# Layer-1 gates by row sums on VectorE, without GpSimd splits and gate sums, and with a shorter closing norm, in a two-layer hybrid block

## The chip, the cores and the metric

The kernel runs on 1 core of one Trainium2 chip. The metric is device time in microseconds (us) of one execution, the median of several runs; smaller is better. PE is TensorE (its matmuls; PEld is its weight loads), DVE is VectorE, ACT is ScalarE, POOL is GpSimd, SP is SyncE, which issues the DMAs here.

## The reference

Two layers over 256 context and 256 latent tokens of width 2048. A layer norms its input, modulates it with a shift and a scale, projects it, mixes it by two branches, projects back, norms again and adds the result times a gate. Shift, scale and gate come from a conditioning vector:

```python
cond_x = jax.nn.silu(c)
for i in range(DEPTH):
    sh_x, sc_x, gt_x = jnp.split(cond_x @ ada_w[i] + ada_b[i], 3, axis=-1)
    u_x = modulate(rms_norm(h_x, pre_g[i]), sh_x, sc_x)
    ...
    h_x = h_x + gt_x[:, None] * rms_norm(out_x, post_g[i])
```

The change touches how `gt_x` of layer 1 is computed (a vector of 2048 times a matrix of 2048 by 2048), where the residues of some weights are made, and the last norm, after which `h_x` is the output. Only the latent tokens are needed at the end of layer 1.

## The kernel before

Every large product is done as three matmuls of a split pair: a tile of weights (`raw`, 512 KB, 128 partitions by 1024 floats) is rounded to `wh` by ACT (line 73), the residue `wl` is made by DVE (line 76), and PE runs high by high, high by low, low by high (`mm3`, and line 469 in `group`). `group` takes eight such tiles of weights, one per pair of K blocks, from `next_w`, which keeps three ready. `raw` has four buffers, and every tile of conditioning weights (`ada`) shares them.

After each K pair `group` calls a step function, which pushes background work one step on: generators for the conditioning (`ada_steps`, `ada_vec`), for attention (`att`) and for the state-space branch (`s5q`). The order in which the engines get their instructions is made by the scheduler of the language from this program order and its own estimate of times, with `tc.high_priority()` as a hint; each engine then runs its list strictly in order.

The conditioning matrices are cut into 12 blocks of 512 columns for each layer, block q 8 to 11 being the gate. Three ways are in use:

- `ada_steps` on PE: the conditioning vector is the stationary side, the matrix streams through (line 143).
- `ada_vec` with `eng` V: DVE multiplies each K tile with its scalar and adds (line 387), PE sums over partitions at the end (line 398).
- `ada_vec` with `eng` G: ACT multiplies in place in the `raw` buffer (line 392), POOL adds (line 393), then the same sum on PE. Layer 1's gate blocks 9 to 11 go this way (line 1303); block 8 goes by `ada_steps` (line 909).

The places in order of time: layer 0 up to its last projection (`wo0`, four passes n4, lines 898 to 926); its last pass runs in two halves, t 0 and 1, then t 2 and 3, each followed by `mid_chain` (line 860), which norms the tokens on DVE and ACT so that the projections of layer 1 can start (`u1_pair`). In the second half of that pass five of the eight `wl` residues are made by POOL (lines 302 and 314). Then layer 1: one group for the state-space input, and from line 1318 six iterations over pairs of heads, each a group `kv` and a group `aq`/`ag` (in the first iteration `kv` ran earlier), with attention of the pair before and the state-space branch as background; `step1` (line 1305) runs the POOL generator from the second iteration on, and `step_ada` two times in three. A last projection (`adg`), then the closing stage: four passes of 512 columns over two token tiles (lines 1381 to 1393), the sums of squares on ACT, the gate product on DVE, and after the last pass `token_rsqrt` (line 850) and four updates with their output DMAs for each token tile.

Of the kernel before, what the change touches and what calls it, by code (L numbers as in the profile page):

```python
# [10 lines left out]
F32 = mybir.dt.float32  # L11
# [7 lines left out]
P = 128  # L19
# [21 lines left out]
def tile_backbone(ctx: ExitStack, tc: tile.TileContext, a):  # L41
# [225 lines left out]
    for q in range(8):  # L267
# [23 lines left out]
        for kt in (2 * q, 2 * q + 1):  # L291
# [7 lines left out]
    wsrc = [(a["w0"][i, kp], 512) for i in range(7) for kp in range(8)]  # L299
    wsrc += [(a["w0t"][kp], P) for kp in range(8)]  # L300
    wsrc += [(a["w0"][7, kp], 512) for kp in range(8)]
    wsrc += [(a[nm][i, kp], 512) + ((G,) if nm == "wo0" and n == 4 and kp in range(2, 7) else ())
             for nm, order in (("wo0", (0, 1, 2, 3, 3)),
                               ("w1", (0, 0) + tuple(range(1, 14))), ("wo1", (0, 1, 2, 3)))
             for n, i in enumerate(order) for kp in range(8)]
    wready = []

    def load_w(src, n, slo=V):
        w = wpool.tile([P, 2, 512], F32, tag="raw", name="raw", bufs=4)
        wh = wpool.tile([P, 2, 512], F32R, tag="wh", name="wh", bufs=3)  # L310
        wl = wpool.tile([P, 2, 512], F32R, tag="wl", name="wl", bufs=3)
        w, wh, wl = w[:, :, 0:n], wh[:, :, 0:n], wl[:, :, 0:n]
        nc.sync.dma_start(w, src)
        split(w, wh, wl, slo=slo)
        return wh, wl

    def fill_w(n):
# [51 lines left out]
            ada_finish(epool[0], l, q, es, epool[1])  # L369
            ada_done(l, (q,))  # L370

    def ada_vec(l, qs, nm, pool, eng):

        accs = []
        for i, q in enumerate(qs):
            accs += [pool.tile([P, 512], F32, tag="pa%d" % (i * nm + m), name="pa")
                     for m in range(nm)]
            for kp in range(8):
                w = wpool.tile([P, 2, 512], F32, tag="raw", name="raw", bufs=4)
                k0 = 2 * (kp % 2)  # L380
                nc.sync.dma_start(w, a["ada%d" % l][q, kp // 2][:, k0:k0 + 2, :])
                for kt, m in ((2 * kp + j, m) for j in range(2) for m in range(nm)):
                    acc, wj, c = accs[i * nm + m], w[:, kt % 2, :], condS[:, kt, m:m + 1]
                    if kt == 0:
                        S.activation(acc, wj, AF.Copy, scale=c)
                    elif eng is V:
                        V.scalar_tensor_tensor(acc, wj, c, acc, ALU.mult, ALU.add)  # L387
                    else:
                        pr = wj
                        if m < nm - 1:  # L390
                            pr = scr.tile([P, 512], F32, tag="t512", name="pr")
                        S.activation(pr, wj, AF.Copy, scale=c)  # L392
                        eng.tensor_tensor(acc, acc, pr, ALU.add)  # L393
                yield
        n = 32 * len(accs)
        E = psp.tile([P, 512], F32, tag="ps", name="Ep")
        for g, acc in enumerate(accs):
            T.matmul(E[32 * g:32 * g + 32, :], ones[:, 0:32], acc, start=True, stop=True,
                     skip_group_check=True)
        es = scr.tile([P, 512], F32, tag="t512", name="es")  # L400
        S.activation(es[0:n], E[0:n], AF.Copy)
        yield
        pt = psp.tile([P, 4, n], F32, tag="ps", name="ept")
        for b in range(4):
            T.transpose(pt[:, b, :], es[0:n, b * P:(b + 1) * P], ident[0:n, 0:n])
        for i, q in enumerate(qs):
            lo = COLS["adab"][0] + 48 * l + 4 * q
            V.tensor_tensor(
                ada[l][:, 4 * q:4 * q + 4, 0:nm],
                pt.rearrange("p b (q m r) -> p q r b m", q=len(qs), m=nm)[:, i, 0],  # L410
                cols[:, lo:lo + 4].rearrange("p (b o) -> p b o", o=1).to_broadcast([P, 4, nm]),
                ALU.add)
        ada_done(l, qs)

    gates = [0, 0]

    def ada_done(l, qs):
        for q in qs:
            if q < 8:
                mod_cols(l, q)  # L420
            else:
                gates[l] += 1
                if gates[l] == 4:
                    gate_rows(l, *epool)

    def run(q, n=1):
        while q and n > 0:
# [318 lines left out]
    kts = list(range(KT))  # L746
    for l, qs in ((0, range(8, 12)), (1, range(8))):
        ada_bg.append(ada_steps(l, [q for q in qs if (l, q) not in ((1, 5), (1, 6), (1, 7))]))
        pool_bg += [ada_vec(l, (q,), 2, l0, V) for q in qs if (l, q) in ((1, 5), (1, 6), (1, 7))]

    def step0():
        step_ada()
# [153 lines left out]
    pump(1e9)  # L906
    run(ada_bg, 1e9)
    run(pool_bg, 1e9)
    ada_bg.append(ada_steps(1, range(8, 12 - 3)))
    out0_open(3)  # L910
    pairs = iter(())

# [70 lines left out]
    ustr = lambda kt, j: (uh[kt].rearrange("p (c j) -> p j c", j=4)[:, j, :],  # L983
                          ul[kt].rearrange("p (c j) -> p j c", j=4)[:, j, :])
    accs, blocks = tblocks(ustr)
    group(kts, blocks, step=step_ada)
    U = l1.tile([P, 16, P], F32, tag="U", name="U")
    D2 = [l1.tile([P, 4, 4, 32], F32, tag=tg, name="D2" + tg) for tg in ("PT", "bias", "qT", "sg")]
    for j in range(4):
# [310 lines left out]
    s5q += [s5_inputs(), s5_pairs(), s5_glu()]  # L1300
    qs = P ** -0.5

    pool_bg = [ada_vec(1, tuple(range(12 - 3, 12)), 1, l1, G)]

    def step1():
        if hp_ >= 1:
            run(pool_bg)
        step_ada()
        run(att)
        run(s5q)  # L1310

# [34 lines left out]
    for k in KORD1[:2]:  # L1346
# [5 lines left out]
    while ada_bg:  # L1352
        step_ada()
    run(pool_bg, 1e9)
    run(s5q, 1e9)
    run(att, 1e9)
    for k in KORD1[2:8]:
# [16 lines left out]
    for c, tg in enumerate(("uh14", "ul14", "uh15", "ul15")):  # L1374
# [3 lines left out]
    oF = [[o0[:, c, :] for c in range(4)],  # L1378
          [l1.tile([P, 512], F32, tag=tg, name="o1" + tg) for tg in ("bias", "qT", "sg", "VT")]]
    ssf = l1.tile([P, 2, 4], F32, tag="ssf", name="ssf")  # L1380
    for n4 in range(4):
        accs = [acc_tile("ao%d" % t) for t in range(2)]
        group(KORD1, [blk(accs[t], 0, 512, sta=lambda k, t=t: ntok(k, t)) for t in range(2)],
              tail=3 if n4 == 3 else 1)
        for t in range(2):
            jk = scr.tile([P, 512], F32, tag="t512", name="jk")
            S.activation(jk, accs[t], AF.Square, accum_out=ssf[:, t, n4:n4 + 1])
            V.tensor_tensor(oF[t][n4], accs[t], g1[n4], ALU.mult)
            if n4 == 3:
                r = token_rsqrt(ssf[:, t:t + 1, :], 1, "rf%d" % t, "rf")  # L1390
                for c in range(4):
                    V.scalar_tensor_tensor(hx[t][c], oF[t][c], r, hx[t][c], ALU.mult, ALU.add)
                    nc.sync.dma_start(a["out"][t][:, 512 * c:512 * c + 512], hx[t][c])
# [3 lines left out]
def _ct(x):  # L1397
    return np.ascontiguousarray(x)
# [18 lines left out]
def _layout(inp):  # L1417
# [29 lines left out]
    for l in range(2):  # L1447
        aw = inp["ada_w"][l].reshape(4, 4, P, 6144)
        out = np.empty((12, 4, P, 4, 512), np.float32)
        for q in range(12):  # L1450
            out[q] = aw[:, :, :, qcols[q]].transpose(0, 2, 1, 3)
        o["ada%d" % l] = out
    w = inp["ab_w_in"][0]
    gv = lambda *cs: sum([[1024 + P * c, P * c] for c in cs], [])
    bg = lambda *cs: [4096 + P * c for c in cs]
# [59 lines left out]
```

## Time and profile before

| | |
|---|---|
| Time, median of 3 runs (lowest, highest) | 1566.83 us (1566.81, 1566.91) |
| The profiled execution's own time | 1562.3 us |
| Its span | 1560.5 us |
| Mean granted TensorE clock | 0.986 of full |
| Busy share of the span: DVE, ACT, POOL | 66%, 38%, 15% |
| Moved by DMA | 268.83 MB, mean 172 GB/s |

The span runs from the first to the last instruction; the execution's own time is 1.8 us longer. The profiled execution was 4.5 us faster than the median of the runs. Durations below are of this one execution.

### The profile page before, as it was taken

The page shows a single profiled execution, that of the slowest core. Times are in us where ns is not written, and L with a number is a line of the kernel's source. Part 1 is how long each engine was busy: PE and PEld are TensorE (multiplying, and loading weights), DVE is VectorE, ACT ScalarE, POOL GpSimd, SP SyncE. Part 2 cuts the span into 40 slices and gives each one's busy share as a digit, 9 for nine tenths or more (in the row PEclk, how much of TensorE's full clock was granted, in tenths as well). Part 3 has the DMA queues.
Part 4 walks back from the last instruction along what each step waited for, and adds up shares of the span by engine and source line. Part 5 has one row for each costly group of instructions (what it writes and reads, how often), then busy time and mean ns, then how long its engine had stood idle before and what let it go on. Part 6 is the DMA issues. An engine that isn't in the chain of part 4 may idle for free.

```text
span 1560.5 us, 22281 instructions
## 1 busy us (share of the span) xinstructions
PE 1476.7 (95%) x8306; PEld 1192.1 (76%) x8306; DVE 1026.0 (66%) x2364; ACT 599.0 (38%) x1162; POOL 241.2 (15%) x229
## 2 busy tenths in 40 slices
PE   3999999999999999999989998879999999999996
PEld 2557767777867767787669997668888979889884
DVE  5244999999675456554376638679597785635645
ACT  4222112122234133322358435664463554424542
POOL 0000000010030000000030116774243343100000
PEclk9999999999999999999999999989999999999998
DMA  9985444455344666654574445553232332425653
GB/s 388 359 319 210 162 162 160 164 174 171 122 154 155 205 229 215 209 169 135 188 248 139 149 142 178 188 166 119 75 126 85 112 102 88 142 81 176 229 190 108
DMA packets 74940, 268.83 MB, mean 172 GB/s; under 512 B 8352, under 2 KB 11984, under 8 KB 70096
## 3 DMA queue, kind: packets, MB, share of 16 engines
q1 hardware_dynamic: 74832, 267.42, 49.7%
q8 instruction: 65, 1.06, 0.3%
q14 instruction: 43, 0.35, 0.1%
HBM read 263.16 MB, written 4.22 MB: 171 GB/s over the span
## 4 chain that ended last, share of the span: by engine, by line
PE 71%; DVE 16%; DMA 6%; ACT 3%; issue 2%; POOL 2%; SPq 0%; DVEq 0%; ACTq 0%; POOLq 0%
PE acc L469 31%; PE kv L469 11%; PE ao L469 7%; DMA raw<-in_ada_dram 5%; PE E L143 5%; DVE wl L76 3%; PE acc L204 2%; PE aq L469 2%; PE ag L469 2%; PE acc L205 2%; PE adg L469 1%; PE acc L203 1%; PE po L1271 1%; POOL pa L393 1%; ACT wh L73 1%
## 5 line engine op out<-in xcount | busy, mean ns | idle before, releaser
L73 ACT ACTIVATE wh<-raw 128x1024 fp32r<-128x1024 f32 (+1 forms) x264 | 274.2, 1039 | 584.0 <-PE acc L469 254.8
L76 DVE TENSOR_TENSOR wl<-raw,wh 128x1024 fp32r<-128x1024 f32 (+1 forms) x259 | 324.5, 1255 | 231.0 <-ACT wh L73 230.3
L504 DVE SCALAR_TENSOR_TENSOR cv<-ain,cw,cv 128x512 f32<-128x512 f32 x240 | 170.1, 748 | 0.0
L469 PE MATMUL acc<-uh,wh 128*128 128x512 f32 x400 | 159.6, 399 | 1.6 <-ACT wh L73 1.1
L469 PE MATMUL acc<-uh,wl 128*128 128x512 f32 x400 | 155.3, 392 | 2.3 <-DVE wl L76 2.3
L469 PE MATMUL acc<-ul,wh 128*128 128x512 f32 x400 | 156.1, 390 | 0.0
L469 PE MATMUL kv<-wh,uh 128*128 128x256 f32 x384 | 109.3, 285 | 1.9 <-DVE sg L1316 1.9
L469 PE MATMUL kv<-wl,uh 128*128 128x256 f32 x384 | 109.3, 285 | 0.0
L469 PE MATMUL kv<-wh,ul 128*128 128x256 f32 x384 | 109.3, 285 | 0.0
L387 DVE SCALAR_TENSOR_TENSOR pa<-raw,condS,pa 128x512 f32<-128x512 f32 x90 | 63.2, 747 | 66.7 <-DMA raw<-in_ada_dram 60.8
L469 PEld LDWEIGHTS acc<-uh,wh 128*128 128x128 f32 x400 | 75.0, 188 | 38.9 <-ACT wh L73 10.0
L469 PEld LDWEIGHTS acc<-uh,wl 128*128 128x128 f32 x400 | 75.1, 188 | 20.4 <-DVE wl L76 2.7
L469 PEld LDWEIGHTS acc<-ul,wh 128*128 128x128 f32 x400 | 75.2, 188 | 15.5 <-issue 0.8
L469 PE MATMUL kv<-uh,wh 128*128 128x512 f32 (+1 forms) x224 | 85.8, 386 | 1.0 <-ACT uh L894 1.0
L469 PE MATMUL kv<-uh,wl 128*128 128x512 f32 (+1 forms) x224 | 81.7, 366 | 1.2 <-DVE wl L76 1.2
L469 PE MATMUL kv<-ul,wh 128*128 128x512 f32 (+1 forms) x224 | 81.0, 363 | 0.0
L393 POOL TENSOR_TENSOR pa<-pa,raw 128x512 f32<-128x512 f32 x45 | 65.9, 1467 | 87.3 <-ACT raw L392 84.8
L469 PEld LDWEIGHTS kv<-wh,uh 128*128 128x128 f32 x384 | 73.9, 192 | 4.3 <-DVE sg L1316 2.6
L469 PE MATMUL acc<-wh,mh 128*128 128x512 f32 x192 | 75.4, 395 | 1.6 <-DVE oG L848 1.6
L469 PE MATMUL acc<-wh,uh 128*128 128x512 f32 x192 | 76.1, 398 | 0.0
L469 PE MATMUL acc<-wl,uh 128*128 128x512 f32 x192 | 75.6, 394 | 0.0
L469 PE MATMUL acc<-wh,ul 128*128 128x512 f32 x192 | 75.5, 393 | 0.0
(393 smaller groups left out, 3440.2 us busy)
## 6 DMA issues: line engine op xcount, KB each, us to landing
raw<-in_w_dram SPq DMA_DIRECT2D x184, 512.0 KB, 3.4
raw<-in_ada_dram SPq DMA_DIRECT2D x128, 512.0 KB, 4.6
raw<-in_wo_dram SPq DMA_DIRECT2D x72, 512.0 KB, 3.4
aw<-in_ada_dram SPq DMA_DIRECT2D x32, 1024.0 KB, 7.0
w<-in_w0a_dram SPq DMA_DIRECT2D x8, 896.0 KB, 6.8
h<-in_h_dram SPq DMA_DIRECT2D x4, 1024.0 KB, 7.8
h0t<-in_h0t_dram SPq DMA_DIRECT2D x16, 256.0 KB, 4.4
bias<-in_bias_dram SPq DMA_DIRECT2D x12, 256.0 KB, 3.6
```

The source lines that it names most:

```text
L73: S.activation(hi, src, AF.Copy)
L76: slo.tensor_tensor(lo, src, hi.bitcast(F32), ALU.subtract)
L143: T.matmul(E[32 * g:32 * g + 32, :], condS[:, kt, :], raw, start=(kt < 4), stop=(kt >= 12), skip_group_check=True)
L203: T.matmul(ps, wh, xh, start=start, stop=False)
L204: T.matmul(ps, wh, xl, start=False, stop=False)
L205: T.matmul(ps, wl, xh, start=False, stop=stop)
L387: V.scalar_tensor_tensor(acc, wj, c, acc, ALU.mult, ALU.add)
L393: eng.tensor_tensor(acc, acc, pr, ALU.add)
L469: T.matmul(out, lt, rt, start=st and m == 0, stop=en and m == 2, skip_group_check=True)
L504: ins = V.scalar_tensor_tensor(o, x[:, :, k:k + L], cw05[:, ch, k:k + 1], o, ALU.mult, ALU.add)
L1271: T.matmul(po, vT[:, k, i * P:(i + 1) * P], U_["PT"][:, k, :], start=k == 0, stop=k == 3)
```

## The change

- Layer 1's gate no longer goes by `ada_steps` and `ada_vec`. The gate's weights are laid out with the 2048 output columns along partitions (16 blocks of 128) and the conditioning rows along the free axis, in two halves of 1024 (`ada1g`). For each half, the conditioning vector is spread over all partitions by one DMA (`crow`), and for each of 16 blocks one DVE instruction multiplies a `raw` tile with it and sums each row into one column of `gs`. That makes 32 loads of 512 KB and 32 DVE instructions of 128 by 1024, each with a read of its accumulator. The bytes stay the same: four blocks of 4 MB before, 32 of 512 KB after.
- The conditioning vector is written as a row to DRAM once, when layer 0's gates are ready (`cond_row`).
- `step1` runs `gate_sums` on every second step from the third iteration over heads on. The remaining part of it and `gate_rows` run after the `adg` group is listed.
- The block of gate 8 that PE did during the last pass of layer 0 goes, and the five POOL residues there are made by DVE.
- In the closing stage the sums of the first three passes and EPS are added ahead; the factor 1/D goes into the square; `rsqrt1` has two instructions in each round instead of three; squares, gate products and `rsqrt1` have high priority.

```diff
-    wsrc += [(a[nm][i, kp], 512) + ((G,) if nm == "wo0" and n == 4 and kp in range(2, 7) else ())
+    wsrc += [(a[nm][i, kp], 512)
...
-    def load_w(src, n, slo=V):
+    def load_w(src, n):
...
-        split(w, wh, wl, slo=slo)
+        split(w, wh, wl)
...
-                        pr = wj
-                        if m < nm - 1:
-                            pr = scr.tile([P, 512], F32, tag="t512", name="pr")
-                        S.activation(pr, wj, AF.Copy, scale=c)
-                        eng.tensor_tensor(acc, acc, pr, ALU.add)
...
+    def cond_row(psp, tag="ps"):
+
+        pc_ = psp.tile([16, P], F32, tag=tag, name="pct")
+        cc = scr.tile([P, KT], F32, tag="t512", name="cc")
+        V.tensor_copy(cc, condS[:, :, 0])
+        T.transpose(pc_, cc, ident)
+        cr = sp.tile([32, P], F32, tag="gr", name="cr")[0:16]
+        S.activation(cr, pc_, AF.Copy)
+        nc.sync.dma_start(crowd.rearrange("m (k f) -> (m k) f", f=P), cr)
+
+    def gate_sums(pool):
+
+        gs = pool.tile([P, 2, 16], F32, tag="gs", name="gs")
+        for hf in range(2):
+            cr = pool.tile([P, 1024], F32, tag="crow", name="crow")
+            nc.sync.dma_start(cr, crowd[0:1, 1024 * hf:1024 * hf + 1024].to_broadcast([P, 1024]))
+            for b in range(16):
+                w = wpool.tile([P, 2, 512], F32, tag="raw", name="raw", bufs=4)
+                w = w.rearrange("p j f -> p (j f)")
+                nc.sync.dma_start(w, a["ada1g"][hf, b])
+                V.tensor_tensor_reduce(w, w, cr, 1.0, 0.0, ALU.mult, ALU.add,
+                                       accum_out=gs[:, hf, b:b + 1])
+                yield
+        g = ada[1][:, 32:48, 0]
+        lo = COLS["adab"][0] + 80
+        V.tensor_tensor(g, gs[:, 0, :], gs[:, 1, :], ALU.add)
+        V.tensor_tensor(g, g, cols[:, lo:lo + 16], ALU.add)
+        gate_rows(1, psp)
...
-    ada_bg.append(ada_steps(1, range(8, 12 - 3)))
...
-    group(kts, blocks, step=step_ada)
+    group(kts, blocks)
...
-    pool_bg = [ada_vec(1, tuple(range(12 - 3, 12)), 1, l1, G)]
+    gate_bg = [gate_sums(l1)]
 
     def step1():
-        if hp_ >= 1:
-            run(pool_bg)
-        step_ada()
+        turns[0] += 1
+        if hp_ >= 2 and turns[0] % 2:
+            run(gate_bg)
...
+    def rsqrt1(v, v2, nm):
+
+        t, y, n_ = (l1.tile([P, 1], F32, tag=nm + x, name=nm + x) for x in "tyn")
+        V.tensor_scalar(n_, v, v2, None, ALU.add)
+        V.tensor_scalar(t.bitcast(I32), n_.bitcast(I32), 1, None, ALU.logical_shift_right)
+        V.tensor_scalar(y.bitcast(I32), t.bitcast(I32), -1, 0x5F3759DF, ALU.mult, ALU.add)
+        V.tensor_scalar(n_, n_, -0.5, None, ALU.mult)
+        for _ in range(3):
+            V.scalar_tensor_tensor(t, y, n_, y, ALU.mult, ALU.mult)
+            V.scalar_tensor_tensor(y, t, 1.5, y, ALU.add, ALU.mult)
+        return y
...
-            S.activation(jk, accs[t], AF.Square, accum_out=ssf[:, t, n4:n4 + 1])
-            V.tensor_tensor(oF[t][n4], accs[t], g1[n4], ALU.mult)
+            with tc.high_priority():
+                S.activation(jk, accs[t], AF.Square, scale=D ** -0.5,
+                             accum_out=ssf[:, t, n4:n4 + 1])
+                V.tensor_tensor(oF[t][n4], accs[t], g1[n4], ALU.mult)
+            if n4 == 2:
+
+                V.tensor_reduce(pre[:, t:t + 1], ssf[:, t, 0:3], axis=AX.X, op=ALU.add)
+                V.tensor_scalar(pre[:, t:t + 1], pre[:, t:t + 1], EPS, None, ALU.add)
             if n4 == 3:
-                r = token_rsqrt(ssf[:, t:t + 1, :], 1, "rf%d" % t, "rf")
+                with tc.high_priority():
+                    r = rsqrt1(ssf[:, t, 3:4], pre[:, t:t + 1], "rf%d" % t)
...
+    o["ada1g"] = _ct(inp["ada_w"][1][:, 4096:].reshape(2, 1024, 16, P).transpose(0, 2, 3, 1))
```

The scheduler makes a new order from this. Three places of it matter. First, DVE from the moment the first two token tiles of layer 0's last pass are done (oG with ao are their gate products, r2t, r2n and r_0 the norm's small steps, oG with h0t the token updates). Before, from the end of the first small steps:

```order
L855 TENSOR_SCALAR ms<-sm 128x2
L85 TENSOR_SCALAR r2t<-ms 128x2
L87 TENSOR_SCALAR r2n<-ms 128x2
L86 TENSOR_SCALAR r_0_5743<-r2t 128x2
L89 TENSOR_TENSOR r2t<-r_0_5743 128x2
L90 TENSOR_TENSOR r2t<-r2t,r2n 128x2
L91 SCALAR_TENSOR_TENSOR r_0_5743<-r2t,r_0_5743 128x2
...
L869 SCALAR_TENSOR_TENSOR oG_5532<-oG_5532,r_0_5743,h0t 128x512
L869 SCALAR_TENSOR_TENSOR oG_5735<-oG_5735,r_0_5743,h0t 128x512
L129 TENSOR_REDUCE ada_79<-ept 128x8
```

The same place on DVE with the change:

```order
L881 TENSOR_SCALAR ms<-sm 128x2
L85 TENSOR_SCALAR r2t<-ms 128x2
L87 TENSOR_SCALAR r2n<-ms 128x2
L76 TENSOR_TENSOR wl<-raw,wh 128x1024
L86 TENSOR_SCALAR r_0_5716<-r2t 128x2
...
L91 SCALAR_TENSOR_TENSOR r_0_5716<-r2t,r_0_5716 128x2
L76 TENSOR_TENSOR wl<-raw,wh 128x1024
...
L895 SCALAR_TENSOR_TENSOR oG_5540<-oG_5540,r_0_5716,h0t 128x512
L895 SCALAR_TENSOR_TENSOR oG_5708<-oG_5708,r_0_5716,h0t 128x512
L76 TENSOR_TENSOR wl<-raw,wh 128x1024 x3
L879 TENSOR_REDUCE sm<-ssq 128x2
```

Two residues that POOL made now stand between the small steps of the norm, and three behind the eight token updates.

Second, the DMAs that SP issues in layer 1. Before, in the second iteration over heads:

```order
L381 DMA raw<-in_ada_dram 128x1024 x2
L313 DMA raw<-in_w_dram 128x1024
L381 DMA raw<-in_ada_dram 128x1024
L313 DMA raw<-in_w_dram 128x1024
L381 DMA raw<-in_ada_dram 128x1024 x2
L1233 DMA bias<-in_bias_dram 128x512
L313 DMA raw<-in_w_dram 128x1024
```

With the change, about the middle of the loads for the gate:

```order
L430 DMA raw<-in_ada1g_dram 128x1024
L313 DMA raw<-in_w_dram 128x1024 x2
L426 DMA crow<-crowd 128x1024
L430 DMA raw<-in_ada1g_dram 128x1024
L313 DMA raw<-in_w_dram 128x1024 x2
L1258 DMA bias<-in_bias_dram 128x512
```

In place of one or two loads for the gate per load of weights there is one per two loads of weights, spread over four iterations, and the second `crow` is between them once.

Third, DVE at the end, behind the gate product of the last pass and token tile (rf0 and rf1 are the norms of the two token tiles). Before, the second token tile's rounds stand behind the first one's four updates:

```order
L1392 SCALAR_TENSOR_TENSOR hxkT<-o_13394,rf_13997,hxkT 128x512 x2
L1392 SCALAR_TENSOR_TENSOR hxvT<-o_13394,rf_13997,hxvT 128x512 x2
L85 TENSOR_SCALAR rft<-ms 128x1
L86 TENSOR_SCALAR rf_14027<-rft 128x1
L89 TENSOR_TENSOR rft<-rf_14027 128x1
L90 TENSOR_TENSOR rft<-rft,rfn 128x1
L91 SCALAR_TENSOR_TENSOR rf_14027<-rft,rf_14027 128x1
```

With the change:

```order
L1414 SCALAR_TENSOR_TENSOR rf0t<-rf0y,rf0n 128x1
L1414 SCALAR_TENSOR_TENSOR rf1t<-rf1y,rf1n 128x1
L1415 SCALAR_TENSOR_TENSOR rf0y<-rf0t,rf0y 128x1
L1415 SCALAR_TENSOR_TENSOR rf1y<-rf1t,rf1y 128x1
L1435 SCALAR_TENSOR_TENSOR hxkT<-o_13305,rf0y,hxkT 128x512 x2
L1414 SCALAR_TENSOR_TENSOR rf1t<-rf1y,rf1n 128x1
L1435 SCALAR_TENSOR_TENSOR hxvT<-o_13305,rf0y,hxvT 128x512 x2
L1415 SCALAR_TENSOR_TENSOR rf1y<-rf1t,rf1y 128x1
```

The two tiles' rounds now alternate, and two steps of the second stand between the first one's updates.

## Rows read from the trace of the kernel before

**Rows 1.** The page, part 1: busy us (share of the span) and instructions.

```profile
PE 1476.7 (95%) x8306; PEld 1192.1 (76%) x8306; DVE 1026.0 (66%) x2364; ACT 599.0 (38%) x1162; POOL 241.2 (15%) x229
```

**Rows 2.** Busy time by stretch: us, PE, PEld, DVE, ACT, POOL, clock, DMA, GB/s.

```profile
949.00:1067.40 118.40, 98.46 (x643) 84.30 (x641) 91.17 (x251) 71.71 (x166) 76.08 (x62) 0.91 0.53 176
1067.40:1157.90 90.50, 89.57 (x643) 79.93 (x641) 72.11 (x257) 43.83 (x125) 33.42 (x35) 1.00 0.28 92
1157.90:1250.00 92.10, 90.41 (x646) 79.99 (x644) 72.66 (x256) 45.81 (x130) 34.15 (x35) 1.00 0.30 101
1250.00:1341.40 91.40, 89.70 (x641) 79.44 (x638) 67.15 (x211) 44.78 (x120) 32.92 (x33) 1.00 0.31 103
1341.40:1426.60 85.20, 85.20 (x569) 77.11 (x568) 33.99 (x60) 27.86 (x40) 2.93 (x2) 1.00 0.37 125
```

**Rows 3.** Waits of PE, 935 to 1100 us: total, times, longest.

```profile
PE pt L1264 <- DVE Pm L1255: 7.6, 3, 5.9
PE Ep L398 <- POOL pa L393: 5.5, 1, 5.5
PE po L1271 <- ACT PT L1265: 3.4, 1, 3.4
```

**Rows 4.** Waits of PE, 1158 to 1250 us.

```profile
PE pt L1264 <- DVE Pm L1255: 1.4, 1, 1.4
```

**Rows 5.** The chain that ended last, 752 to 830 us: start, us, what.

```profile
751.54 0.98 PE E L143 x4
...
784.97 1.01 PE E L143 x4
```

**Rows 6.** Tile ao, 752 to 812 us: ns min/median/max, first and last start.

```profile
L469 PE MATMUL ao<-wh,ml x64: 387/389/628, 753.0 to 808.9; 128*128 128x512 f32 x64
...
  POOL wl L76: 3.8, 2
```

**Rows 7.** The chain that ended last, closing stage.

```profile
1458.31 86.04 PE ao L469 x379
```

**Rows 8.** POOL and DVE in order of time around the middle: start, us.

```profile
784.79 7.26 POOL L76 TENSOR_TENSOR wl<-raw,wh 128x1024 fp32r<-128x1024 f32 x3 [340.12 <-ACT wh L73]
...
792.57 2.27 DVE L91 SCALAR_TENSOR_TENSOR r<-r2t,r 128x2 f32<-128x2 f32 x1
...
796.05 7.51 DVE L869 SCALAR_TENSOR_TENSOR oG<-oG,r,h0t 128x512 f32<-128x512 f32 x8
...
815.12 5.39 DVE L869 SCALAR_TENSOR_TENSOR oG<-oG,r,h0t 128x512 f32<-128x512 f32 x8
```

**Rows 9.** Three forms on DVE: count, ns min/median/max, first and last start.

```profile
L557 DVE CUSTOM_DVE_ANT_0 jk<-X x16: 414/419/1509, 352.9 to 449.1; 128x256 f32<-128x256 f32 x16
L557 DVE DVE_READ_ACCUMULATOR2_ANT ssb<- x16: 76/81/83, 353.2 to 449.4; 128x1 f32 x16
...
L76 DVE TENSOR_TENSOR nl<-m,nh x16: 417/422/1519, 995.9 to 1466.1; 128x256 fp32r<-128x256 f32 x16
```

**Rows 10.** Tile wl, 1067 to 1342 us.

```profile
L76 DVE TENSOR_TENSOR wl<-raw,wh x48: 1187/1216/1592, 1068.5 to 1340.1; 128x1024 fp32r<-128x1024 f32 x48
```

**Rows 11.** Busy time by stretch, the groups aq/ag of three iterations.

```profile
1128.70:1157.90 29.20, 29.20 (x257) 27.75 (x251) 28.79 (x106) 18.03 (x53) 9.10 (x9) 1.00 0.36 116
...
1221.00:1250.00 29.00, 29.00 (x253) 27.65 (x248) 28.59 (x105) 17.84 (x52) 9.03 (x9) 1.00 0.36 118
...
1313.00:1341.40 28.40, 28.40 (x249) 27.29 (x246) 23.68 (x64) 16.93 (x42) 7.75 (x7) 1.00 0.41 129
```

**Rows 12.** DVE in order of time, the end.

```profile
1548.82 1.42 DVE L1392 SCALAR_TENSOR_TENSOR hxkT<-o,rf,hxkT 128x512 f32<-128x512 f32 x2
...
1551.48 0.15 DVE L85 TENSOR_SCALAR rft<-ms 128x1 int32<-128x1 int32 x1
...
1553.59 0.75 DVE L1392 SCALAR_TENSOR_TENSOR hxPT<-o1bias,rf,hxPT 128x512 f32<-128x512 f32 x1
```

**Rows 13.** Waits of all engines, the whole span.

```profile
DVE pa L387 <- DMA raw<-in_ada_dram: 60.8, 19, 6.2
```

More of the change, by code (lines that the diff above doesn't have):

```diff
@@ L301, in tile_backbone @@
     wsrc += [(a["w0"][7, kp], 512) for kp in range(8)]
-    wsrc += [(a[nm][i, kp], 512) + ((G,) if nm == "wo0" and n == 4 and kp in range(2, 7) else ())
+    wsrc += [(a[nm][i, kp], 512)
              for nm, order in (("wo0", (0, 1, 2, 3, 3)),
                                ("w1", (0, 0) + tuple(range(1, 14))), ("wo1", (0, 1, 2, 3)))
-             for n, i in enumerate(order) for kp in range(8)]
+             for i in order for kp in range(8)]
     wready = []
-    def load_w(src, n, slo=V):
+    def load_w(src, n):
         w = wpool.tile([P, 2, 512], F32, tag="raw", name="raw", bufs=4)
@@ L370, in ada_steps, with ada_vec @@
             ada_done(l, (q,))
-    def ada_vec(l, qs, nm, pool, eng):
+    def ada_vec(l, qs, nm, pool):
         accs = []
@@ L385, in ada_vec @@
                         S.activation(acc, wj, AF.Copy, scale=c)
-                    elif eng is V:
+                    else:
                         V.scalar_tensor_tensor(acc, wj, c, acc, ALU.mult, ALU.add)
-                    else:
-                        pr = wj
-                        if m < nm - 1:
-                            pr = scr.tile([P, 512], F32, tag="t512", name="pr")
-                        S.activation(pr, wj, AF.Copy, scale=c)
-                        eng.tensor_tensor(acc, acc, pr, ALU.add)
                 yield
@@ L413, in ada_vec @@
         ada_done(l, qs)
+    crowd = dps.tile([1, D], F32, name="crowd")
+    def cond_row(psp, tag="ps"):
[23 more added lines that the diff above has]
+        gate_rows(1, psp)
     gates = [0, 0]
@@ L424, in ada_done @@
                     gate_rows(l, *epool)
+                    cond_row(*epool)
     def run(q, n=1):
@@ L748, in tile_backbone @@
         ada_bg.append(ada_steps(l, [q for q in qs if (l, q) not in ((1, 5), (1, 6), (1, 7))]))
-        pool_bg += [ada_vec(l, (q,), 2, l0, V) for q in qs if (l, q) in ((1, 5), (1, 6), (1, 7))]
+        pool_bg += [ada_vec(l, (q,), 2, l0) for q in qs if (l, q) in ((1, 5), (1, 6), (1, 7))]
     def step0():
@@ L1351, in tile_backbone @@
                first=i % 2 == 0) for i in range(4)], step=step1)
-    while ada_bg:
-        step_ada()
-    run(pool_bg, 1e9)
+    run(gate_bg, 1e9)
     run(s5q, 1e9)
@@ L1380, in tile_backbone @@
     ssf = l1.tile([P, 2, 4], F32, tag="ssf", name="ssf")
+    pre = l1.tile([P, 2], F32, tag="pre", name="pre")
+    def rsqrt1(v, v2, nm):
[8 more added lines that the diff above has]
+        return y
     for n4 in range(4):
```

## The prediction

> **What bounds the kernel now.** I read the busy shares first. PE works 95% of the span, DVE 66% and POOL 15% [rows 1]: the order of work is built around PE, so time can only come from places where PE stands still, runs at its lower clock level or does work that the change takes out. Next the busy time by stretch finds these places [rows 2]. Four iterations over heads do nearly the same matmuls (643, 643, 646 and 641), yet the first takes 118.4 us and the next three 90.5, 92.1 and 91.4. The reader is to see in the first one's row POOL at 76.08 us instead of some 34, ACT at 71.71 instead of some 45, DVE at 91.17 instead of some 72, and a granted clock of 0.91. The waits of PE in that stretch say what held it: probabilities from DVE 7.6 us, a GpSimd gate sum 5.5 us, transposed probabilities from ACT 3.4 us [rows 3]; in the next iteration one such wait of 1.4 us is left [rows 4]. The rest is the clock: at 0.91 over 118.4 us, 118.4 x 0.09 = 10.7 us are lost to stretches at the lower of the two levels, 1.2 GHz. Waits and clock make 16.5 + 10.7 = 27.2 us, which is what this iteration is longer than the others. Last, the chain that ended last is PE in the middle, with eight pieces of layer-1 gate work (E) of about 0.98 us in it [rows 5], and PE again in the closing stage [rows 7].
>
> **The change, part by part.** The sum is made against the profiled execution's own 1562.3 us, which is 4.5 us under the median of 1566.83; I put the difference on the median.
>
> *Layer 0's last pass.* It goes from the first E piece at 751.54 [rows 5] to its last matmul at 808.9 + 0.39 = 809.3 [rows 6], 57.75 us. The 64 groups of three matmuls need at the pace of the closing stage 86.04/379 = 0.227 us each [rows 7], 192 x 0.227 = 43.6 us. The excess is 14.1 us: 8 x 0.98 = 7.8 us of E, which goes; two waits of PE for a residue from POOL, 3.8 us [rows 6], which go; the other 2.5 us, switching between the two kinds of work and what the waits bring with them, go with them. Against that DVE makes five residues more, 5 x 1.22 = 6.1 us by the price of such a residue [rows 10]. Two of them stand in the norm's small steps (2.4 us), but there POOL's residues had held DVE: one small step took 2.27 us beside POOL's, and the eight updates 7.51 us, where the next eight took 5.39 [rows 8], so this is even. One residue that PE needs stands behind eight updates, 5.4 us late at most; PE has other tiles ready for part of it, and I take half, +2.7. That is **-11.4**, between -8.7 (all 5.4 us waited) and -14.1.
>
> *First iteration over heads.* With POOL's sums and ACT's products gone it is like its neighbours: 118.4 to 91.3, the mean of the next two, **-27.1** (-26.3 to -27.9 by the neighbour chosen). What is late next is the same probabilities' wait, 1.4 us in the neighbour [rows 4], and it is in its time already. The gate's loads go out of this iteration too (DMA share 0.53 against 0.28 [rows 2]); the later ones have that room.
>
> *Closing norm.* The second token tile's small steps start at 1551.48 and its last update at 1553.59: 2.1 us in a row between the first tile's updates and the second's [rows 12]. With alternating rounds they go, and with the sums done ahead the first chain is a few steps of 0.15 us shorter; two of the second tile's steps between the first one's updates give 0.3 back. **-2.4** (-1.5 to -3).
>
> *Conditioning row.* One copy, one transpose, one small evacuation on ACT and one DMA, on PE's path at most some issue time: +0.3 (0 to 1).
>
> *Row sums.* This is the price. 32 instructions on DVE of 128 by 1024 with two inputs and an accumulator read. The trace has no such instruction. The nearest ones: an instruction of 256 wide with an accumulator takes 0.419 us, a plain two-input one of that width 0.422, so the summing itself costs nothing, and the read of the accumulator 0.08 [rows 9]; the plain one of 1024 takes 1.22 [rows 10]. So 1.22 + 0.08 = **1.30 us** each, eight per iteration, 10.4 us. Over a whole iteration there is room: 90.5 - 72.11 = 18.4, 92.1 - 72.66 = 19.4, 91.4 - 67.15 = 24.3 and 85.2 - 33.99 = 51.2 us [rows 2]. But half of them lie in the aq/ag groups, and these have none: DVE is busy 28.79 us of 29.2 in the second iteration, 28.59 of 29.0 in the third and 23.68 of 28.4 in the fourth [rows 11]. Four reductions there are 5.2 us, so 4.8, 4.8 and 0.5 run over. Since the matmuls wait for the residues that the same DVE makes, I let PE pay all of it: **+10.1**. The ends: nothing, if the three tiles kept ready carry PE over to the kv group, whose DVE has room; and 24 x 1.30 = 31.2 us, if every reduction of the three full iterations lands on the path. The eight in the last iteration are free in all cases: they lie beside 51 us of idle DVE, and the gate is then done over an iteration ahead of its use. Their loads take the place of as many bytes of before, one 512 KB load per two loads of weights, at a DMA share of 0.3; I cost them at nothing, with the low share as cover, and come back to the case without it.
>
> One thing speaks against this part. In the middle the trace shows DVE's small step of two inputs at 2.27 us beside a chain of POOL's residues [rows 8]; POOL still works 34 us of 92 in the iterations where the reductions go, 35 instructions of 0.98 us [rows 2]. A reduction that finds POOL busy (0.37 of the time) and waits half an instruction (0.49) would add 24 x 0.37 x 0.49 = 4.4 us, and the time would be 1540.7. But the 48 residues of the same form beside the same POOL work are at 1.187, 1.216 and at most 1.592 us [rows 10]; they hardly show it, so the sum goes by 1.30. (The Trainium skill, SBUF — State Buffer, section Who interferes with whom, says that a VectorE instruction with both inputs in SBUF takes turns with a GpSimd instruction that reads SBUF, each locking the other out for its whole length. By that rule the 1540.7 holds; the small step of 2.27 us agrees with it, the median of the 48 residues does not.)
>
> Sum: -11.4 - 27.1 - 2.4 + 0.3 + 10.1 = -30.5. From the own time 1531.8; on the median, 1566.83 - 30.5 = **1536.3 us**. All low ends give -14.1 - 27.9 - 3 = -45, 1521.8; all high ends -8.7 - 26.3 - 1.5 + 1 + 31.2 = -4.3, 1562.5.
>
> **Rivals.**
>
> *All reductions on the path.* DVE is the bound in both groups of an iteration, because residues, attention and updates come in an order that leaves it no slack where a reduction stands. For it: the first iteration, where 91.17 us of DVE in 118.4 already held PE [rows 2, 3]. Against: 18 us free in each iteration. 31.2 in place of 10.1: 1557.4.
>
> *The change doesn't do what it says.* The first iteration's wait for probabilities and for ACT come from the attention chain itself, not from POOL: then only the 5.5 us of the gate sum go [rows 3], -5.5 in place of -27.1: 1557.9. For it: those waits name DVE and ACT. Against: the neighbour has the same chain and 1.4 us of it [rows 4].
>
> *Less than the forecast's price.* The tiles ready carry the overrun, and the sum goes with 0 there and low ends elsewhere: 1522 to 1526.
>
> *Slower: DVE waits for the loads.* A reduction stands in DVE's list, strictly in order; if its tile hasn't landed, the residues behind it wait too, and PE with them. The tiles share four buffers with the weights, so a load can only start when a buffer comes free. The conditioning work that DVE does during layer 0, with loads of the same size, waited for them 60.8 us in 19 waits, 3.2 us each [rows 13]. At that price DVE needs 211.9 + 24 x (1.3 + 3.2) = 319.9 us in three iterations of 274.0 together [rows 2], +45.9 in place of +10.1: 1572.1. It decides from a wait of 2.98 us per reduction (274.0 + 40.6 = 211.9 + 24 x 4.28). For it: the same sharing of buffers. Against: a DMA share of 0.3 where the reductions go, one such load per two weights, and the 60.8 us lie where DVE may have had time to wait.
>
> **How the numbers follow.** The forecast, with a share of its overrun paid, has 0.60; all on the path 0.16; waits that stay 0.07; the better case 0.07; the slower case 0.10, of which 0.02 end near no change, since its price runs through that point. About 0.2%, 3.1 us, is what a measurement of this kernel can tell from no change. The range goes from the sum of the low ends, 1522, to the two middle cases, 1558; it leaves out the slower case and a little beyond the ends. Faster 0.90, same 0.02, slower 0.08.
>
> **What would show it.** Right: no E and no POOL residue between 750 and 810, and that pass some 11 us shorter; the first iteration near 91 us at a granted clock of 1.00 with no GpSimd wait; 32 reductions of 1.2 to 1.3 us on DVE; the second to fourth iterations together some 10 us longer, PE's added waits there naming residues or probabilities from DVE, in the aq/ag groups; the last iteration as before; the last update some 2.4 us sooner after the last matmul. Wrong: DVE waiting for the gate's loads by more than 1 us each; the first iteration still at a clock near 0.9; reductions that take far more than 1.3 us; or a new wait where the five residues went that is more than 5.4 us.

## The result: 1533.3 us, and the profile after

| | before | with the change |
|---|---|---|
| Time, median | 1566.82 us | 1533.3 us (1529.52 to 1535.49, 4 runs) |
| Ratio | | 0.978, 95% interval 0.9765 to 0.980 |
| Profiled execution: own time, span | 1562.3, 1560.5 us | 1529.5, 1527.5 us |
| Granted TensorE clock, mean | 0.986 | 0.993 |

The forecast was 1536.3 us. That it came so close is in part luck, because two of its steps were wrong in opposite directions: one term was 10 us too dear, and a loss of some 11 us was missing. The busy time by stretch shows it. I cut both spans at the same eight places of the program: the start of layer 0's last pass (with its first piece of gate work before), its last matmul, the start of the iteration with `hp_` = 1 (the one that the prediction calls first), of that with `hp_` = 2, of the last with `hp_` = 5, of the closing passes, their last matmul, the end. Columns are us, PE, PEld, DVE, ACT, POOL, clock, DMA share, GB/s. The kernel before:

```profile
0.00:751.50 751.50, 714.52 (x3413) 519.29 (x3413) 497.26 (x978) 205.23 (x298) 26.12 (x34) 1.00 0.57 202
751.50:809.30 57.80, 56.00 (x229) 37.91 (x228) 31.28 (x47) 24.92 (x41) 11.91 (x5) 0.97 0.70 231
809.30:949.00 139.70, 133.94 (x926) 132.97 (x925) 82.52 (x180) 78.24 (x161) 22.33 (x24) 0.99 0.47 157
...
1067.40:1341.40 274.00, 269.69 (x1923) 239.37 (x1922) 211.91 (x721) 134.43 (x372) 100.50 (x101) 1.00 0.30 99
1341.40:1458.20 116.80, 116.80 (x801) 106.37 (x800) 57.45 (x110) 45.71 (x74) 4.30 (x3) 1.00 0.40 135
1458.20:1545.50 87.30, 87.26 (x385) 71.86 (x384) 44.26 (x46) 38.08 (x50) 0.00 (x0) 1.00 0.54 185
1545.50:1560.50 15.00, 0.00 (x0) 0.00 (x0) 10.10 (x38) 0.69 (x2) 0.00 (x0) 0.57 0.42 140
```

The changed kernel, the same view and places (the fourth row answers to the first of [rows 2]):

```profile
0.00:760.50 760.50, 725.21 (x3412) 521.41 (x3413) 497.62 (x979) 205.27 (x299) 26.27 (x34) 1.00 0.57 199
760.50:806.60 46.10, 44.86 (x195) 36.21 (x194) 31.58 (x59) 24.45 (x40) 0.00 (x0) 1.00 0.63 210
806.60:946.90 140.30, 134.41 (x925) 133.85 (x923) 78.06 (x172) 73.87 (x153) 9.55 (x15) 0.98 0.44 146
946.90:1035.10 88.20, 87.90 (x629) 78.60 (x627) 68.69 (x242) 43.47 (x118) 27.54 (x27) 1.00 0.28 97
1035.10:1309.30 274.20, 268.78 (x1927) 238.70 (x1926) 243.94 (x767) 136.67 (x378) 116.08 (x101) 1.00 0.45 149
1309.30:1425.90 116.60, 116.60 (x802) 105.97 (x801) 68.64 (x134) 45.73 (x75) 4.19 (x3) 1.00 0.53 175
1425.90:1515.40 89.50, 89.46 (x386) 72.13 (x384) 44.83 (x52) 38.07 (x51) 0.00 (x0) 1.00 0.53 181
1515.40:1527.50 12.10, 0.00 (x0) 0.00 (x0) 8.39 (x29) 0.68 (x2) 0.00 (x0) 0.62 0.50 173
```

Subtracting row by row: the first stretch +9.0, layer 0's last pass -11.7, the way to `hp_` = 1 +0.6, the iteration `hp_` = 1 -30.2, the three iterations `hp_` = 2 to 4, with most of the row sums, +0.2, the last one with `adg` -0.2, the closing passes +2.2, the end -2.9: -33.0 in all. Three rows gain as said (layer 0's last pass, `hp_` = 1, the end), one costs nothing where 10.1 was forecast, and two lose where PE's work is the same: 3413 and 3412 matmuls in the first stretch, 385 and 386 in the closing passes, at a granted clock of 1.00 in both kernels. No wait of PE explains it, since PE's *busy* time grew, by 10.7 and 2.2 us.

### The profile page after: what moved, and what is told of

It is laid out like the page before. It is cut to its first block, busy times and chain, and to the rows that moved or that the text cites. A ratio compares the mean times of both kernels' runs of the same rounds, so it can differ in the third digit from the quotient of the medians.

```text
span 1527.5 us, 22085 instructions
## 1 busy us (share of the span) xinstructions
PE 1467.2 (96%) x8261; PEld 1186.9 (78%) x8261; DVE 1041.7 (68%) x2427; ACT 568.2 (37%) x1113; POOL 183.6 (12%) x179
## 4 chain that ended last, share of the span: by engine, by line
PE 79%; DVE 15%; DMA 3%; issue 2%; ACT 1%; SPq 0%; DVEq 0%; ACTq 0%
PE acc L495 35%; PE kv L495 12%; PE ao L495 8%; PE E L143 4%; DVE wl L76 3%; PE aq L495 2%; PE ag L495 2%; PE acc L204 2%; PE acc L205 2%; PE adg L495 1%; PE acc L203 1%; DMA raw<-in_ada1g_dram 1%; PE po L1296 1%; PE Sc L1267 1%; DVE acc L245 1%
## 5 line engine op out<-in xcount | busy, mean ns | idle before, releaser
L495 PE MATMUL acc<-wl,mh 128*128 128x512 f32 x192 | 75.5, 393 | 0.0
```

The costliest lines, as they stand in the source:

```text
L495: T.matmul(out, lt, rt, start=st and m == 0, stop=en and m == 2, skip_group_check=True)
```

## Experiments

### Where the lost 11 us went: the pace of the matmuls

The matmuls of the first stretch tell more when lines are kept apart. Tile wl, two forms of its matmuls from 60 to 720 us (ns min/median/max, first and last start). The kernel before:

```profile
L469 PE MATMUL acc<-uh,wl x400: 387/389/799, 152.4 to 610.4; 128*128 128x512 f32 x134
...
L205 PE MATMUL acc<-uh,wl x89: 388/389/398, 59.9 to 151.8; 128*128 128x512 f32 x89
```

The changed kernel:

```profile
L495 PE MATMUL acc<-uh,wl x400: 388/393/794, 153.3 to 619.3; 128*128 128x512 f32 x134
...
L205 PE MATMUL acc<-uh,wl x91: 387/389/397, 59.9 to 152.6; 128*128 128x512 f32 x91
```

The same form takes 389 ns in both kernels as long as its weights come from the pool of the input projection (line 205), and 393 instead of 389 once they come from the pool that `load_w` fills. What differs there is the place in SBUF. The new closing norm keeps its small tiles in the pool `l1`, and four tiles of 32 bytes leave the pool `sp`, which lies ahead of the scratch and weight pools: the compiled programs put the first raw tile at byte 103936 of each partition before and at 103808 with the change, and the first `wh` at 120320 and 120192.

First both kernels once more, unchanged, on one chip.

> The kernel before once more, unchanged, as the yardstick for the three others, profiled on the same chip. In the two profiles so far the stretch up to layer 0's last pass, where the two kernels do the same work, lasted 719.4 us before and 727.8 with the change, and PE's 512-wide matmuls followed each other at 227 and at 231 ns. Theory, chip or execution: the pace belongs to the profiled execution, so on one chip both kernels have the same stretch within 2 us. Rival, kernel: the change slows that stretch (other addresses in SBUF), and it stays 8 us longer with the change. Time 1567 by both.

> The changed kernel once more, unchanged. Theory, chip or execution: the first stretch is within 2 us of that of the kernel before in this call, and the gain is then about 33 us in the rest alone. Rival, kernel: the first stretch is 8 us longer, the rest gains some 41 us. Time 1530 to 1535 by both.

Medians 1566.24 and 1530.69 us. The first stretch took 753.5 and 762.0 us, the closing passes 87.3 and 89.5. So the pace belongs to the kernel, not to a chip or an execution.

Then the place alone, with the order of instructions on each engine the same as in the changed kernel:

```diff
+    sp.tile([P, 32], F32, tag="pad", name="pad")
     scr = ctx.enter_context(tc.tile_pool(name="scr", bufs=4))
```

> The changed kernel with one unused tile of 128 bytes per partition ahead of the scratch pool, and nothing else. The change drops four small tiles of 32 bytes there (the closing norm's), so its weight tiles start at byte 103808 of a partition, where before they started at 103936; the pad puts them back at 103936. Theory, addresses: PE's slower pace with the change (231 against 227 ns from one 512-wide matmul to the next, the first stretch 9.4 us longer, the closing passes 89.48 against 87.32 us) comes from where the weights lie, so this kernel has 227 ns, 720 us and 87.3 us again and is 10 to 13 us faster than the changed kernel, near 1519. Rival, order or chip: the pace belongs to other instructions of the change, and the pad does nothing (within 3 us of the changed kernel).

1523.33 us (1521.42 to 1527.69), 0.972 of before (0.970 to 0.9745): 7 to 10 us under the changed kernel's two medians. The same view of this kernel, its first stretch, and the closing passes:

```profile
0.00:754.90 754.90, 715.81 (x3412) 519.48 (x3413) 497.06 (x979) 205.19 (x299) 26.25 (x34) 1.00 0.57 201
...
1419.60:1507.20 87.60, 87.58 (x386) 71.90 (x384) 44.75 (x52) 38.07 (x50) 0.00 (x0) 1.00 0.54 185
```

PE's busy time is back at 715.8 and 87.6 us. An unused tile gives back what the change had lost.

> The same with a pad of 64 bytes: the weight tiles start at byte 103872. If the pace hangs on the weights starting at a multiple of 256 bytes, this is as slow as the changed kernel or slower (within 3 us, 1530 to 1536); if it hangs on a multiple of 64, it is as fast as the kernel with 128 (1519); in between, something finer.

1527.12 us (32 becomes 16 in the diff), between the two. Its first stretch and closing passes:

```profile
0.00:760.90 760.90, 721.89 (x3413) 519.41 (x3414) 497.47 (x979) 205.09 (x299) 26.18 (x34) 1.00 0.57 199
...
1423.10:1512.80 89.70, 89.70 (x386) 71.97 (x384) 44.77 (x52) 38.07 (x50) 0.00 (x0) 1.00 0.54 180
```

The closing passes are as slow as in the changed kernel or slower, but in the first stretch PE's 721.9 us lie between the 715.8 with the whole pad and the 725.2 without one, and the aq/ag groups, with 256-wide moving tiles, take 28.0 us against 28.2 to 28.3, a little less. So no single step of 64 or 256 bytes describes it; only these three places were tried.

The same from the other side: the kernel before with the closing norm alone (all of the diff from `rsqrt1` on, but for the `ada1g` array), without and with the pad.

```diff
-                r = token_rsqrt(ssf[:, t:t + 1, :], 1, "rf%d" % t, "rf")
+                with tc.high_priority():
+                    r = rsqrt1(ssf[:, t, 3:4], pre[:, t:t + 1], "rf%d" % t)
```

> The kernel before with the new closing norm alone. The closing norm's small tiles leave their pool here too, so the weights lie at byte 103808. Theory of the prediction: only the closing stage counts, -2.4 us, 1564. Theory, addresses: 2.4 to 2.9 us are gained after the last matmul, and 9 to 12 are lost to PE's pace everywhere else, so this is 7 to 9 us slower than before, 1574.

> The kernel before with the new closing norm and the pad of 128 bytes, so the weights stay at byte 103936. By addresses as by the prediction's term it is 2.4 to 2.9 us faster than before, 1564; only if the closing norm itself costs something elsewhere is it slower.

Without the pad 1575.23 us, ratio 1.0054 (1.0036 to 1.0072); with it 1564.85, 0.998 (0.9964 to 0.9993). The kernel before had a median of 1568.13 on the same chip. So the part of the change with the forecast of -2.4 us costs 7.1 by itself, and with the pad it gains 3.3; the place of the weights is 10.4 us, the difference of the two medians. Busy time by stretch, without the pad:

```profile
0.00:763.30 763.30, 727.32 (x3413) 521.82 (x3415) 497.90 (x978) 204.98 (x298) 26.24 (x34) 0.99 0.57 199
...
1560.40:1573.00 12.60, 0.00 (x0) 0.00 (x0) 8.41 (x29) 0.69 (x2) 0.00 (x0) 0.64 0.48 167
```

and with it:

```profile
0.00:753.40 753.40, 715.63 (x3413) 518.93 (x3415) 497.24 (x978) 204.91 (x298) 26.12 (x34) 1.00 0.57 201
...
1547.00:1559.70 12.70, 0.00 (x0) 0.00 (x0) 8.41 (x29) 0.66 (x2) 0.00 (x0) 0.70 0.47 166
```

The end is shorter in both (15.0 before), the first stretch long in one only. Last, whether it is what PE reads or what the DMAs write that has to lie there:

```diff
         w = wpool.tile([P, 2, 512], F32, tag="raw", name="raw", bufs=4)
+        wpool.tile([P, 32], F32, tag="pad", name="pad")
         wh = wpool.tile([P, 2, 512], F32R, tag="wh", name="wh", bufs=3)
```

> The changed kernel with the pad of 128 bytes not ahead of the scratch pool but between the tiles of raw weights and those of their rounded parts and residues: what PE reads (wh, wl, layer 0's mh, ml) lies where it did before (wh at byte 120320), the raw tiles that the DMAs write and the scratch tiles stay 128 bytes lower (raw at 103808). Theory, PE's reads: the pace hangs on where PE's own operands lie, so this is as fast as the kernel with the pad ahead of everything (1523, first stretch 720 to 723 us, closing passes 87.5 us). Rival, the DMAs' writes: transfers into raw tiles that start off a multiple of 256 bytes disturb PE, so this is as slow as the changed kernel (1531 to 1533, 728 to 730 and 89.5 us).

1522.86 us, 0.972 (0.969 to 0.975), although raw and scratch tiles lie as in the changed kernel:

```profile
0.00:753.60 753.60, 716.25 (x3413) 519.01 (x3413) 497.15 (x979) 205.55 (x299) 26.27 (x34) 1.00 0.57 201
1419.20:1506.80 87.60, 87.55 (x386) 71.88 (x384) 44.75 (x51) 38.12 (x51) 0.00 (x0) 1.00 0.56 185
```

So the tiles from `wh` on upward decide, the ones that PE reads. This kernel and the one with the pad ahead of all beat both given kernels, the changed one by 7 to 10 us and the one before by 44.

### What a row sum costs

> Leaves out the 32 loads of the gate's weights, the 32 row sums and the two spreads of the conditioning row (the gate is the bias alone). Theory of the prediction: the sums overrun DVE's aq/ag groups by 10.1 us that PE pays, so this is 10 us faster than the changed kernel, in the second to fourth iterations over heads. Rival, free: the sums lie in DVE's idle time and the prediction had the 10.1 us wrong; this is within 2 us of the changed kernel. Second rival, all on the path: 31 us faster.

```diff
-            cr = pool.tile([P, 1024], F32, tag="crow", name="crow")
...
-                V.tensor_tensor_reduce(w, w, cr, 1.0, 0.0, ALU.mult, ALU.add,
-                                       accum_out=gs[:, hf, b:b + 1])
+            V.memset(gs[:, hf, :], 0.0)
```

1535.5 us, 0.980 of before (0.978 to 0.983): not faster at all. The three iterations `hp_` = 2 to 4 without the sums:

```profile
1041.30:1315.80 274.50, 270.43 (x1929) 238.71 (x1929) 211.23 (x725) 137.11 (x379) 102.82 (x101) 1.00 0.31 102
```

274.5 us without and 274.2 with 32.7 us more on DVE, with the weights at the same place in both: the sums are free. (The 4.8 us by which its median lies above the repeated changed kernel's come earlier: its last pass of layer 0 starts at 767.8 instead of 762.0. Why is not shown; that stretch differs by as much between kernels whose program is the same up to there, from 751.5 us in the kernel before to 758.8 in its variant with the spread GpSimd sums, below.)

> Every row sum is done twice, over the same loaded tile: 64 instead of 32, 41.6 us more of DVE, 10.4 us more per iteration. Theory of the prediction: the aq/ag groups are full, so each further 5.2 us there comes on top: about 16 us slower than the changed kernel (5.2 x 3, nothing in the last iteration). Rival, free: DVE has 18 us per iteration and PE's ready tiles carry it over the full groups, so 64 cost under 4 us as well. The comparison of the two tells where the room ends.

```diff
                                        accum_out=gs[:, hf, b:b + 1])
+                V.tensor_tensor_reduce(w, w, cr, 1.0, 0.0, ALU.mult, ALU.add,
+                                       accum_out=gx[:, hf, b:b + 1])
```

1546.31 us, 0.987 of before (0.985 to 0.990), 15.6 us over the changed kernel on the same chip. Its iterations `hp_` = 2 to 4:

```profile
1038.40:1131.20 92.80, 90.55 (x646) 79.56 (x645) 84.09 (x266) 45.88 (x128) 38.39 (x34) 1.00 0.43 140
1131.20:1227.10 95.90, 92.30 (x647) 81.11 (x646) 91.21 (x278) 45.31 (x129) 36.80 (x34) 0.98 0.44 141
1227.10:1325.20 98.10, 92.56 (x643) 79.95 (x642) 92.00 (x269) 44.18 (x121) 32.60 (x33) 0.98 0.42 140
```

286.8 us, 12.6 more; the changed kernel's iterations are 91.9, 91.5 and 90.8 us long, with 80 to 82 us of DVE. There nothing is paid; with DVE at 91 to 92 us the second and third of these iterations are 4.4 and 7.3 us longer, a part of the 10 us or so that eight further sums take. PE's waits in the three now name residues from DVE, 5.0 us in all, and probabilities, 3.8 us. The prediction's mechanism exists, one step further on than it was put.

> The changed kernel with the 128-byte pad, and one row sum after every K pair from the second group of the first iteration on, as densely as GpSimd's sums stood before: 32 in one and a half iterations instead of four. 16 sums per iteration are 20.8 us of DVE, where 64 in four iterations (16 each) cost 12 us over three iterations. Theory, room on DVE: two crowded stretches cost some 4 us each, 4 to 10 us slower than the spread sums (1527 to 1533). Rival, engine: what held the iteration was GpSimd and ACT in the chain, not the density, and dense sums on DVE cost under 2 us.

```diff
-        if hp_ >= 2 and turns[0] % 2:
+        if hp_ >= 1:
```

1535.8 us, 0.980 of before (0.9765 to 0.984) and 12.5 us over the spread sums (with the pad in both), more than either theory had. `hp_` = 1 and 2 of this kernel:

```profile
940.40:1032.00 91.60, 88.17 (x625) 78.21 (x623) 77.31 (x243) 42.71 (x115) 28.90 (x26) 1.00 0.53 170
1032.00:1135.60 103.60, 94.69 (x646) 82.06 (x645) 95.10 (x290) 46.26 (x130) 29.93 (x34) 0.97 0.56 178
```

Of the sums 13 lie in the first and 17 in the second, where DVE is at 95.1 of 103.6. Crowded into two iterations the row sums cost 12.5 us; GpSimd's way of the kernel before cost 30. So the spread is a part of what the change gains. The loads are crowded here too: DVE waited 15.4 us for them in the two iterations, and the run does not separate that from the sums themselves.

> The kernel before with its gate sums left on ACT and GpSimd, but pushed on every second step from the third iteration over heads, as the change does with its row sums, instead of every step from the second. Theory, engine: GpSimd's sums slow DVE and hold raw buffers wherever they run, so the stalls move to later iterations and no more than 10 of the 27 us of the first iteration are gained (1556 to 1568). Rival, density: the first iteration was only too crowded; spread out, ACT and GpSimd are nearly free and some 20 to 27 us are gained (1540 to 1547).

```diff
-        if hp_ >= 1:
+        turns[0] += 1
+        if hp_ >= 2 and turns[0] % 2:
             run(pool_bg)
```

1569.21 us, 1.0016 (0.9994 to 1.0038): no gain. The edit did less than was expected of it: `step_ada`, which `step1` still calls, pushes the same sums itself, two times in three and from the first iteration on, and the edit left that in. So 21 of 45 lie in `hp_` = 1 and 17 in `hp_` = 2, where before 36 lay in the first alone. Those two iterations:

```profile
954.20:1059.00 104.80, 93.53 (x632) 83.20 (x630) 81.27 (x248) 59.87 (x147) 56.34 (x48) 0.93 0.46 152
1059.00:1169.20 110.20, 95.75 (x659) 84.18 (x655) 89.83 (x262) 58.74 (x151) 56.64 (x52) 0.92 0.38 126
```

104.8 + 110.2 = 215.0 us against 118.4 + 90.5 before [rows 2]: at about half the density they cost no less, 35 us over the changed kernel's 88.2 and 91.9. So for this engine half the density gained nothing. What a thinner spread over four iterations would do was not tried, and the rival of the density is only in part answered.

### Residues alone

> The kernel before with only the five residues of layer 0's last pass moved from GpSimd to DVE; PE's eight pieces of gate work stay. By the prediction's terms: two waits of PE for GpSimd's residue go (3.8 us) and what came with them (up to 2.5), a wait of 2.7 us behind eight updates comes: between -1 and -4 us, 1563 to 1566. Rival: the residues in DVE's norm chain delay the start of layer 1 and it is 2 us or more slower.

```diff
-    wsrc += [(a[nm][i, kp], 512) + ((G,) if nm == "wo0" and n == 4 and kp in range(2, 7) else ())
+    wsrc += [(a[nm][i, kp], 512)
```

1562.23 us, 0.997 (0.9945 to 0.9996). Its last pass and its iteration `hp_` = 1, then PE's waits from the start of that pass to 830 us:

```profile
756.20:810.80 54.60, 53.99 (x228) 36.78 (x226) 30.08 (x55) 24.65 (x41) 0.00 (x0) 1.00 0.73 247
949.60:1070.40 120.80, 98.07 (x643) 85.20 (x641) 100.33 (x251) 71.36 (x167) 73.76 (x62) 0.92 0.52 172
```

```profile
PE z L885 <- DVE dg L875: 3.7, 1, 3.7
PE ao L469 <- DVE wl L76: 0.6, 1, 0.6
```

57.8 us become 54.6, as the terms said (-1 to -4). The changed kernel's pass is 46.1 us, and 45.4 with the pad, which has the weights at the same place as here. So the E pieces, with the switching that goes with them, are worth the other 9.2 us, for which the prediction had 7.8 and a part of 2.5. The iteration `hp_` = 1 still takes 120.8 us at a clock of 0.92: the residues have no part in what the change gains there.

## Why the prediction was near, step by step

**Layer 0's last pass: right.** -11.4 said, -11.7 measured. The feared wait behind eight updates, 2.7 us, was 1.2 in the changed kernel (PE's waits, 760 to 830 us):

```profile
...
PE ao L495 <- DVE wl L76: 1.2, 1, 1.2
```

At its slower pace the pass is still as short as said, and 45.4 us with the pad.

**The first of the four iterations: right, a little small.** -27.1 said, -30.2 measured. POOL went from 76.1 to 27.5 us, ACT from 71.7 to 43.5, DVE from 91.2 to 68.7 and the granted clock from 0.91 to 1.00. PE's waits from 930 to 1100 us in the changed kernel:

```profile
PE pt L1289 <- DVE Ce L688: 1.8, 1, 1.8
PE kv L495 <- DVE sg L1341: 0.4, 1, 0.4
PE pt L1289 <- DVE Pm L1280: 0.3, 1, 0.3
```

against 16.5 us in [rows 3]. It came out below its neighbours since PE has less to do there, 629 matmuls against 643 in the neighbour [rows 2], and is busy 87.9 of 88.2 us; before, 11 matmuls of the gate were among its 643. The prediction took the neighbours' length for it and so put this term 3.1 us too small: some 2 us are PE's smaller share of work, 1 us is idle time that the neighbours have. The rival in which these waits stay is out.

**The row sums: the step that failed.** The price of one was right: 1.30 us said. Line 431 of the changed kernel, its instructions (count, ns min/median/max, first and last start) and what DVE sat idle for ahead of them (us, times):

```profile
L431 DVE CUSTOM_DVE_ANT_0 raw<-raw,crow x32: 1187/1226/1646, 1035.3 to 1387.6; 128x1024 f32<-128x1024 f32 x32
L431 DVE DVE_READ_ACCUMULATOR2_ANT gs<- x32: 72/82/84, 1036.4 to 1388.8; 128x1 f32 x32
...
  DMA raw<-in_ada1g_dram: 20.5, 17
```

What failed is "Four reductions there are 5.2 us, so 4.8, 4.8 and 0.5 run over" and "I let PE pay all of it": +10.1 us said, +0.2 measured in the three iterations, and no wait of PE for a residue in them. It took the aq/ag groups as full and the sums as added to them. DVE's time on line 431 in the kv and the aq/ag group of `hp_` = 2 (a sum counts twice, with its read):

```profile
1035.10:1098.70 63.60, 7.58 (x12) 1.00 0.42 136
1098.80:1127.00 28.20, 2.44 (x4) 1.00 0.51 171
```

Six of the eight sums lie in the kv group, two in the aq/ag group, and all of DVE's work in the latter (the view of the first fences):

```profile
1098.80:1127.00 28.20, 28.20 (x246) 27.28 (x245) 26.72 (x94) 17.43 (x49) 10.29 (x8) 1.00 0.51 171
```

is less than the 28.79 us of before [rows 11], with two sums in it: of the 106 instructions there before 90 are left, and the sums with their reads make four of the 94. Over the three iterations the aq/ag groups have 38 instructions other than sums fewer than before and the kv groups, which had room, 35 more. A busy share of 98% in a group was not a limit, but work that could as well lie elsewhere. The room to count was rather that of the iteration, 18 us: 10 us of sums cost nothing there, and twice as many, 20 us, do not fit.

**The rule on the shared port.** The sums took 1.226 us in the median and 1.646 at most with GpSimd at 38 to 40 us per iteration, and nothing reached PE, so the 1540.7 is out. The residues in `hp_` = 1, beside GpSimd's 76 us before (first line) and its 27.5 us now (second):

```profile
L76 DVE TENSOR_TENSOR wl<-raw,wh x18: 1207/1272/2332, 947.1 to 1062.7; 128x1024 fp32r<-128x1024 f32 x18
L76 DVE TENSOR_TENSOR wl<-raw,wh x15: 1190/1215/1521, 947.4 to 1033.0; 128x1024 fp32r<-128x1024 f32 x15
```

The Trainium skill (SBUF — State Buffer, Who interferes with whom) says that a VectorE instruction with two inputs in SBUF contends with a GpSimd instruction that reads SBUF. These residues agree with it in direction, by 57 ns in the median; how much one such meeting costs, these runs don't show.

**The slower rival.** DVE does wait for the gate's loads, 20.5 us in 17 waits, the longest 3.6; that is 0.6 us per sum against the 2.98 from which it would have decided. A wait that does occur is 1.2 us long on average, more than the 1 us that the prediction named as a sign of being wrong, and still PE paid nothing.

**The closing norm: right after the last matmul, wrong as a whole.** -2.4 said for it, -2.9 measured (15.0 to 12.1 us). The step left out that its tiles' new pool moves every weight tile; in these two profiles the stretches that show it are 9.0 + 2.2 us longer, and the pairs of medians with and without the pad differ by 7.4 and 10.4 us. Nothing in the prediction holds this. With the row sums at nothing it would have forecast 1526.2, and the padded kernel, which has no loss of pace, took 1523.33; with the 11.2 us of lost pace added, 1537.4 for the changed kernel as it stands. The 1536.3 was near because the two errors of some 10 us cancelled.

**The conditioning row.** +0.3 said; it lies in the first stretch, where profiles differ by more than that, so no run here shows it.

## What to carry to other kernels

Compare PE's busy time for the same matmuls before and after an edit: if it grew without a wait, look at where the operands lie, and put allocations back with an unused tile before judging the edit. When background work is moved to an engine, count its room over the longest stretch in which the order may shift, not over the fullest group; and spread it, since the same sums crowded into two iterations cost 12.5 us.

## What was not expected of the hardware

Matmuls with a 512-wide fp32 moving tile take 389 or 393 ns (closing passes 87.3 to 87.6 or 89.5 us for 384 of them), depending on whether the first `wh` tile starts at byte 120320 or at 120192 of a partition. With a 256-wide moving tile it is the other way round, by 2 ns. One form of each from the changed kernel (tiles nl and aq):

```profile
L495 PE MATMUL ao<-wh,nl x128: 390/393/404, 1426.3 to 1515.0; 128*128 128x512 f32 x128
L495 PE MATMUL aq<-uh,wh x192: 276/281/470, 921.3 to 1392.6; 128*128 128x256 f32 x192
```

and from the kernel with the pad ahead of all:

```profile
L496 PE MATMUL ao<-wh,nl x128: 388/389/397, 1420.1 to 1506.8; 128*128 128x512 f32 x128
L496 PE MATMUL aq<-uh,wh x192: 280/283/466, 913.9 to 1386.1; 128*128 128x256 f32 x192
```

So the iterations over heads, where most matmuls are 256 wide, do not show the loss: `hp_` = 2 to 4 take 274.7 us with the pad and 274.2 without.

The weights' place counts on either side of a matmul. In acc<-uh,wl the moving tile `uh` lies in a pool ahead of `sp` and kept its place, so only the stationary `wl` moved, and the 400 matmuls went from 389 to 393 ns. In ao<-wh,nl `wh` is the moving tile, and the stationary `nl` lies at the same bytes in the changed and the padded kernel. The pieces of gate work on PE, with 32 columns of weights, kept 604 ns in both given kernels, although their moving tile (`raw`) had moved as well. Why 128 bytes matter, these runs leave open.
